# A transformer block on one core: the turn of the memory rows, the pace of the later projections, and the output steps behind the heads, in a table that sets the order of the work

## The chip, the cores and the metric

The kernel runs on one core of one Trainium2 chip. The metric is the device time of one execution, in microseconds (us), as the median of several runs. The kernel before took 1988.11 us, the median of 3 runs that lay between 1987.46 and 1988.55 us.

The engines are called as in the profile: PE is TensorE (matmuls), PEld its weight loads, DVE is VectorE, ACT is ScalarE, POOL is GpSimd, and SP is SyncE, which here only issues transfers from the chip's memory. Each engine takes its own instructions strictly in the order in which the program lists them.

## The reference

The reference is a transformer block with attention, cross attention to a memory and a gated feed-forward, then a second model of two more blocks. The change touches the first block's attention alone, which is this, cut to what matters:

```python
h = rmsnorm(x, attn_norm_g)                       # x: 512 tokens x 1024
fq, fk, fv, sq, sk, sv, f_logit = split(h @ w_in) # 8 + 8 heads of 64
log_f = log_sigmoid(f_logit + b_forget)
fox_o = softmax(fq.fk/8 + c[t] - c[s], causal) @ fv      # c = cumsum(log_f)
sb_o  = stick_breaking(sigmoid(sq.sk/8), strictly causal) @ sv
mixed = concat(rmsnorm(fox_o, fox_out_g), rmsnorm(sb_o, sb_out_g))
x = x + mixed @ w_out
h = rmsnorm(x, xattn_norm_g)
m = rmsnorm(mem, mem_norm_g)                      # mem: 256 rows x 1024
k, v = split(m @ w_mkv)                           # keys and values of the memory
x = x + softmax(heads(h @ w_mq).k/16) @ v @ w_mo
```

All of it is float32 in and out, to float32 accuracy.

## The kernel before

To reach that accuracy each float32 operand is split into two parts, high and low: ACT casts the high part (L162 for data, L179 for weights) and DVE subtracts it to get the low part (L163, L180). A product is then three matmuls (high by high, L197; high by low, L198; low by high, L199), called a step here. A step over 512 columns is three matmuls of 512 columns.

The stage that is changed is `mixers`, from about 45 us to 305 us of the span. It has two kinds of work. The first kind is projections, long chains of steps on PE that need little of the other engines: queries and keys of a pair of heads (`qk1` to `qk7`, 16 steps each), the values of the second eight heads (`v`, 32 steps), the keys of the memory (`mk`: two turns that only transpose the memory's rows, normalize and split them, then 32 turns of two steps over 256 columns), the memory's values (`mv`, 32 steps), and the output projection (`out`). The second kind is the sixteen heads, 0 to 7 stick-breaking and 8 to 15 with softmax and forget gates. A head's scores are eight small matmuls (L647, L648, over 128 to 512 columns) into two banks `ps_s`. ACT and DVE turn them into probabilities: for a softmax head DVE adds the bias and takes the maximum (L686), ACT exponentiates (L689), and POOL and DVE scale the rows (L257). Then PE transposes the ten blocks of probabilities (L417) into two banks `ps_t`, ACT and DVE split them again (`ch`, `cl`), and eight matmuls with the values follow (L706, L707) into one bank `ps_o`, which ACT and DVE empty at the end (L711, L712). Of a head the matmuls are short, and the other engines work on it for far longer than PE does.

The order is set by times without a unit. Head number h gives its four score rows between h - 0.68 and h + 0.106 and its products from h + 1.347 on. `FILL` is a list of projections with their number of turns and the time at which each ends, and within an entry the turns lie evenly. `weave` merges all these lanes by time into one program. From it a scheduler builds each engine's list of instructions by its own estimates, and may move an instruction ahead of others whose inputs it thinks late. So the order on an engine follows the table only roughly.

The memory's rows come in by two transfers (L778), issued by SP on the queue that also brings all weights (L174, into two buffers `wst`). Then 16 transposes (L538) put them into banks `ps_f`, of which there are three; the projections write to the same three. DVE scales each bank by the gain (L541) and the result is split. The rows wait for one of 13 large buffers `s8`. ACT squares the rows (L332) for their norms, and `spread` turns the norms into a row (L377 on DVE, L379 on PE). The first keys of the memory follow on PE after L379.

After `weave` the rest of `out` runs. Its last 36 of 64 steps need the softmax heads normalized, and that hangs on the last head: its squares are summed (L346, L347), split, summed over partitions by 8 small matmuls (L356, in `mean_sq`), raised to the power -1/2 on POOL (L319), spread to a row by 8 matmuls (L372), and multiplied in (L732). Meanwhile steps of `out` that need only the stick-breaking heads are there to run.

Of the kernel before, what the change touches and what calls it, by code (L numbers as in the profile page):

```python
# [13 lines left out]
F32R = mybir.dt.float32r  # L14
# [46 lines left out]
def weave(*lanes):  # L61

    heap = [(times[0], i, 0) for i, (times, _) in enumerate(lanes)]
    heapq.heapify(heap)
    while heap:
        t, i, k = heapq.heappop(heap)
        times, gen = lanes[i]
        if next(gen, None) is not None:
            k += 1
            heapq.heappush(heap, (times[min(k, len(times) - 1)], i, k))  # L70


def even(t0, t1, n):
    return [t0 + (i + 0.5) * (t1 - t0) / n for i in range(n)]


def filling(gens, plan, t0):

    times, parts = [], []
    for i, (name, n, t1) in enumerate(plan):  # L80
        times += even(t0, t1, n)
        more = any(name == later[0] for later in plan[i + 1:])
        parts.append(itertools.islice(gens[name], n) if more else gens[name])
        t0 = t1
    return times, itertools.chain(*parts)


def run(gen):
    for _ in gen:
        pass  # L90


FILL = [['qk1', 16, 0.85], ['qk2', 16, 2.1], ['qk3', 16, 3.4], ['v', 32, 5.95], ['qk4', 16, 7.2], ['qk5', 16, 8.5], ['qk6', 16, 9.85],
        ['mk', 2, 10.2], ['qk7', 16, 11.5], ['mk', 32, 13.9], ['mv', 32, 16.4], ['out', 12, 17.3]]
FOX_SCALE = 'pppd'
LATENT_SCALE = 'dpad'
NORM_SB = 14.0
# [9 lines left out]
class Kernel:  # L107
# [231 lines left out]
    def squares(self, acc, src, first):  # L339
# [6 lines left out]
        nc.scalar.activation(sq, src, AF.Square)  # L346
        nc.vector.tensor_add(acc, acc, sq)  # L347

    def mean_sq(self, acc, n, eps=EPS, bank="o"):

        ss = self.ps(bank)
        parts = [self.t2("sq", dt=F32R) for _ in range(2)]
        self.split(*parts, acc)
        for b in range(NB):
            for i, part in enumerate(parts):
                self.nc.tensor.matmul(ss[:, 2 * b:2 * b + 2], lhsT=part[:, b * P:(b + 1) * P], rhs=self.ones_r[:, 0:2],  # L356
                                      start=i == 0, stop=i == 1)
        ms = self.sm(NB)
        self.nc.vector.tensor_scalar(ms, ss[:, 0:2 * NB:2], 1.0 / n, eps, op0=ALU.mult, op1=ALU.add)  # L359
        return ms  # L360
# [355 lines left out]
    def mixers(self):  # L716

        a, nc = self.a, self.nc
        self.qk, self.rows = {}, {}
        cd = self.forget()  # L720
        self.sb_scale = self.scaled_cols(0.125)
        run(self.qk_pair(0))
        mixed, parts, v_fox = {}, {}, []
        accs = [self.t2("acc") for _ in range(2)]

        def split_mixed(kind, row):

            m = mixed[kind]
            parts[kind] = [self.s8([P, 4, T], F32R) for _ in range(2)]
            for pr in range(4):  # L730
                g = self.g[("sb", "fox")[kind]][:, pr:pr + 1]
                nc.vector.scalar_tensor_tensor(m[:, pr], m[:, pr], g, row, op0=ALU.mult, op1=ALU.mult)  # L732
                self.split(*(t[:, pr] for t in parts[kind]), m[:, pr])

        def normed_sb():
            row = self.spread(self.rstd_from(self.mean_sq(accs[0], 512, bank="f"), NB), "f")
            yield 1
            split_mixed(0, row)
            yield 1

        def values_fox():
            v_fox.extend(self.s8([P, NB, 4, 2, 64], F32R) for _ in range(2))
            for block in self.vproj(v_fox, 1024):
                yield from block


        out = self.down(lambda k: tuple(t[:, k % 4] for t in parts[k // 4]), a["w_out"][0], 8,
                        self.boundary(self.g["xattn"], rows=False),
                        [(range(3), range(4)), (range(3, 7), range(4)), (range(3), range(4, 8)), (range(3, 7), range(4, 8)),
                         ([7], range(4)), ([7], range(4, 8))], 2, row=lambda k: (k + 4) % 8)  # L750
        gens = {"mk": self.memory_keys(), "mv": self.memory_values(), "v": values_fox(), "out": itertools.islice(out, 12)}
        gens.update({f"qk{pr}": self.qk_pair(pr) for pr in range(1, 8)})
        lanes = [filling(gens, FILL, -0.4), ([NORM_SB, NORM_SB + 0.3], normed_sb())]
        for hd in range(16):
            kind = hd // 8
            v = (self.v_sb, v_fox)[kind]
            head = self.sb_head(hd) if kind == 0 else self.fox_head(hd, cd)
            lanes.append((even(hd + SCORES[0], hd + SCORES[1], 4), head))
            lanes.append(([hd + MIX_OUT + t for t in ATTEND], self.mix_head(hd, v, mixed, accs[kind])))
        weave(*lanes)  # L760
        self.x = [self.s8([P, 4, T]) for _ in range(2)]
        for h in range(2):
            nc.scalar.dma_start(self.x[h].rearrange("p k t -> p (k t)"), self.x_dram[h])
        run(itertools.islice(out, 7))
        ms = self.mean_sq(accs[1], 512)
        run(itertools.islice(out, 4))
        row = self.spread(self.rstd_from(ms, NB), direct=True)
        run(itertools.islice(out, 5))
        split_mixed(1, row)
        run(out)  # L770

# [603 lines left out]
```

## Time and profile before

| what | us |
|---|---|
| median of 3 runs | 1988.11 |
| profiled execution, its own time | 1992.29 |
| span of the profiled execution | 1990.5 |
| PE busy, of that span | 1955.9 |
| DVE busy | 1124.7 |
| ACT busy | 863.3 |
| POOL busy | 199.5 |

The profiled execution took 4.18 us more than the median of the runs. Its own time is 1.8 us longer than its span.

PE is busy for 98% of the span, and the chain that ended last runs for 94% of the span over PE. That makes PE the engine to follow, but its busy time has to be read with care: matmuls overlap each other, the profile models their ends, and a matmul that stands alone counts as busy for longer than the 0.23 us (512 columns) after which the next one could start. In stretches of short matmuls with waits between them, the busy share therefore hides lost time. Starts are the thing to look at there.

In forty slices of the span the granted PE clock shows 9 tenths or more everywhere. In finer windows the stage `mixers` has a few places where it is lower.

### The profile page before, as it was taken

The page shows a single profiled execution, that of the slowest core. Times are in us where ns is not written, and L with a number is a line of the kernel's source. Part 1 is how long each engine was busy: PE and PEld are TensorE (multiplying, and loading weights), DVE is VectorE, ACT ScalarE, POOL GpSimd, SP SyncE. Part 2 cuts the span into 40 slices and gives each one's busy share as a digit, 9 for nine tenths or more (in the row PEclk, how much of TensorE's full clock was granted, in tenths as well). Part 3 has the DMA queues.
Part 4 walks back from the last instruction along what each step waited for, and adds up shares of the span by engine and source line. Part 5 has one row for each costly group of instructions (what it writes and reads, how often), then busy time and mean ns, then how long its engine had stood idle before and what let it go on. Part 6 is the DMA issues. An engine that isn't in the chain of part 4 may idle for free.

```text
span 1990.5 us, 24467 instructions
## 1 busy us (share of the span) xinstructions
PE 1955.9 (98%) x9205; PEld 1634.4 (82%) x9205; DVE 1124.7 (57%) x1973; ACT 863.3 (43%) x1503; POOL 199.5 (10%) x260
## 2 busy tenths in 40 slices
PE   8999989999999999999999999999999999999998
PEld 7887978888888888888888888888887878888887
DVE  6788866567666533657775533333567764333334
ACT  6677744444333323645354323222446553332223
POOL 1545500001111100001210000000010000000000
PEclk9999999999999999999999999999999999999999
DMA  6323343123333332232223333223231123332332
GB/s 185 96 75 96 107 148 92 52 87 110 96 95 96 99 101 85 87 116 85 72 83 110 109 100 96 95 95 96 71 89 52 51 76 108 95 97 85 98 101 78
DMA packets 216344, 187.24 MB, mean 94 GB/s; under 512 B 12273, under 2 KB 188441, under 8 KB 215713
## 3 DMA queue, kind: packets, MB, share of 16 engines
q1 hardware_dynamic: 213905, 178.32, 30.1%
q10 hardware_dynamic: 2320, 7.36, 1.1%
q8 instruction: 72, 1.18, 0.3%
q14 instruction: 47, 0.39, 0.1%
HBM read 181.44 MB, written 4.21 MB: 93 GB/s over the span
## 4 chain that ended last, share of the span: by engine, by line
PE 94%; DVE 2%; ACT 2%; DMA 1%; issue 1%; POOL 0%; SPq 0%; ACTq 0%; POOLq 0%; DVEq 0%
PE ps_f L197 15%; PE ps_f L198 15%; PE ps_f L199 15%; PE ps_s L197 7%; PE ps_s L198 7%; PE ps_s L199 7%; PE ps_t L197 6%; PE ps_t L198 6%; PE ps_t L199 6%; PE ps_o L198 2%; PE ps_o L199 2%; PE ps_o L197 2%; PE ps_t L417 1%; ACT wh L179 0%; PE ps_s L647 0%
## 5 line engine op out<-in xcount | busy, mean ns | idle before, releaser
L179 ACT CAST wh<-wst 128x1024 fp32r<-128x1024 f32 (+4 forms) x349 | 344.1, 987 | 674.9 <-PE ps_f L198 317.9
L180 DVE TENSOR_TENSOR wl<-wst,wh 128x1024 fp32r<-128x1024 f32 (+4 forms) x349 | 401.2, 1150 | 325.7 <-ACT wh L179 319.6
L197 PE MATMUL ps_f<-s,wh 128*128 128x512 f32 (+1 forms) x892 | 344.0, 391 | 5.0 <-ACT s L162 2.5
L198 PE MATMUL ps_f<-s,wh 128*128 128x512 f32 (+1 forms) x892 | 344.7, 387 | 0.0
L199 PE MATMUL ps_f<-s,wl 128*128 128x512 f32 (+1 forms) x892 | 343.0, 386 | 0.0
L197 PEld LDWEIGHTS ps_f<-s,wh 128*128 128x128 f32 x892 | 168.8, 190 | 38.3 <-ACT s L162 2.9
L199 PEld LDWEIGHTS ps_f<-s,wl 128*128 128x128 f32 x892 | 169.2, 190 | 32.8 <-issue 0.2
L198 PEld LDWEIGHTS ps_f<-s,wh 128*128 128x128 f32 x892 | 169.5, 190 | 31.2 <-issue 0.5
L319 POOL TENSOR_TENSOR sm<-sm,m_half 128x1 f32<-128x1 f32 (+1 forms) x31 | 26.5, 855 | 1253.8 <-DVE sm L359 824.0
L162 ACT CAST ch<-s 128x512 fp32r<-128x512 f32 (+1 forms) x166 | 77.4, 496 | 154.1 <-PE ps_s L198 100.2
L163 DVE TENSOR_TENSOR cl<-s,ch 128x512 fp32r<-128x512 f32 (+1 forms) x166 | 85.8, 536 | 86.7 <-ACT ch L162 86.4
L197 PE MATMUL ps_s<-s,wh 128*128 128x512 f32 x288 | 112.8, 393 | 0.3 <-ACT wh L179 0.3
L198 PE MATMUL ps_s<-s,wh 128*128 128x512 f32 x288 | 112.4, 390 | 0.0
L199 PE MATMUL ps_s<-s,wl 128*128 128x512 f32 x288 | 111.8, 389 | 0.0
L197 PE MATMUL ps_t<-s,wh 128*128 128x512 f32 x280 | 109.4, 392 | 0.0
L198 PE MATMUL ps_t<-s,wh 128*128 128x512 f32 x280 | 109.1, 389 | 0.0
L199 PE MATMUL ps_t<-s,wl 128*128 128x512 f32 x280 | 108.3, 389 | 0.0
L198 PE MATMUL ps_f<-cl,wh 128*128 128x512 f32 x210 | 82.1, 391 | 0.0
L199 PE MATMUL ps_f<-ch,wl 128*128 128x512 f32 x210 | 81.8, 389 | 0.0
L197 PE MATMUL ps_f<-wh,s 128*128 128x512 f32 (+2 forms) x208 | 75.6, 374 | 3.5 <-ACT s L162 3.0
L198 PE MATMUL ps_f<-wl,s 128*128 128x512 f32 (+2 forms) x208 | 76.0, 369 | 1.0 <-DVE wl L180 1.0
L197 PE MATMUL ps_f<-ch,wh 128*128 128x512 f32 x210 | 76.4, 390 | 0.0
(452 smaller groups left out, 3902.2 us busy)
## 6 DMA issues: line engine op xcount, KB each, us to landing
wst<-in_mlp_w SPq DMA_DIRECT2D x128, 512.0 KB
wst<-in_w_up SPq DMA_DIRECT2D x44, 512.0 KB
wst<-in_a_w_in SPq DMA_DIRECT2D x32, 512.0 KB
wst<-in_w_in SPq DMA_DIRECT2D x23, 512.0 KB
wst<-in_w_down SPq DMA_DIRECT2D x22, 512.0 KB
wst<-in_w_mkv SPq DMA_DIRECT2D x16, 512.0 KB
wst<-in_a_w_out SPq DMA_DIRECT2D x16, 320.0 KB
wst<-in_w_mq SPq DMA_DIRECT2D x8, 512.0 KB
```

Of the source, the lines that this page charges most:

```text
L162: nc.scalar.copy(hi, src)
L163: nc.vector.tensor_sub(lo, src, hi.bitcast(F32))
L179: self.nc.scalar.copy(h[:, j], st[:, j])
L180: self.nc.vector.tensor_sub(l[:, j], st[:, j], h[:, j].bitcast(F32))
L197: mm(out, lhsT=ah, rhs=bh, start=first, stop=False)
L198: mm(out, lhsT=ah, rhs=bl, start=False, stop=False)
L199: mm(out, lhsT=al, rhs=bh, start=False, stop=last)
L319: self.nc.gpsimd.tensor_tensor(r, ms, self.m_half[:, 0:n], op=ALU.pow)
L417: self.nc.tensor.transpose(pt[:, i * P:(i + 1) * P], probs[i][:, j * P:(j + 1) * P], self.ident)
```

## The change

The table `FILL` is changed in four ways. The two turns that take in the memory's rows stood after `qk6` and before `qk7`; now they stand after `qk7`, at the head of the memory's keys (`mk`, 34 turns). The pairs end later: `qk5` at 8.8 instead of 8.5, `qk6` at 10.35 instead of 9.85, `qk7` at 11.8 instead of 11.5. The memory's keys end at 14.2, its values at 16.6. Of the output steps 8 instead of 12 lie among the heads, so that 20 instead of 16 lie behind them.

In the code behind `weave` the split of the last sum of squares is written ahead of the first of these steps (`split_acc`), and the steps come in pieces of 8, 6 and 6 instead of 7, 4 and 5.

```diff
-FILL = [['qk1', 16, 0.85], ['qk2', 16, 2.1], ['qk3', 16, 3.4], ['v', 32, 5.95], ['qk4', 16, 7.2], ['qk5', 16, 8.5], ['qk6', 16, 9.85],
-        ['mk', 2, 10.2], ['qk7', 16, 11.5], ['mk', 32, 13.9], ['mv', 32, 16.4], ['out', 12, 17.3]]
+FILL = [['qk1', 16, 0.85], ['qk2', 16, 2.15], ['qk3', 16, 3.5], ['v', 32, 6.1], ['qk4', 16, 7.3], ['qk5', 16, 8.8], ['qk6', 16, 10.35],
+        ['qk7', 16, 11.8], ['mk', 34, 14.2], ['mv', 32, 16.6], ['out', 8, 17.3]]
...
-    def mean_sq(self, acc, n, eps=EPS, bank="o"):
-
-        ss = self.ps(bank)
+    def split_acc(self, acc):
         parts = [self.t2("sq", dt=F32R) for _ in range(2)]
         self.split(*parts, acc)
+        return parts
+
+    def mean_sq(self, acc, n, eps=EPS, bank="o"):
+
+        ss = self.ps(bank)
+        parts = acc if isinstance(acc, list) else self.split_acc(acc)
...
-        run(itertools.islice(out, 7))
-        ms = self.mean_sq(accs[1], 512)
-        run(itertools.islice(out, 4))
+        acc = self.split_acc(accs[1])
+        run(itertools.islice(out, 8))
+        ms = self.mean_sq(acc, 512)
+        run(itertools.islice(out, 6))
         row = self.spread(self.rstd_from(ms, NB), direct=True)
-        run(itertools.islice(out, 5))
+        run(itertools.islice(out, 6))
```

Lines of the changed kernel behind `mean_sq` are 4 or 5 higher: its L542, L651, L652, L710, L711, L421 and L383 are the L538, L647, L648, L706, L707, L417 and L379 of before.

On PE, in the kernel before, the last of the 16 transposes of the memory's rows has passed and `qk7` begins (its steps read the normalized input, here `s_105` and `s_107`), between rows of two heads:

```order
L647 MATMUL ps_s<-s_1526 128x512
L648 MATMUL ps_s<-s_1526,ql 128x512
L707 MATMUL ps_o<-cl,s_111 128x128
L417 MATMUL ps_t<-ident_r,pp 128x128 x5
L647 MATMUL ps_s<-s_1717 128x128
L648 MATMUL ps_s<-s_1717,ql 128x128
L706 MATMUL ps_o<-ch,s_1130 128x512
L197 MATMUL ps_f<-s_105,wh 128x512
L198 MATMUL ps_f<-s_107,wh 128x512
L199 MATMUL ps_f<-s_105,wl 128x512
```

The rows down to L706 are the last of 79 matmuls and transposes in a row without a projection (two heads and the memory's rows). From L197 on `qk7`'s 48 matmuls lie among the rows of the next head, and then come 25 of a head without a projection, the first L379 as the last of them.

On PE, in the changed kernel, the end of `qk7` (reading `s_106`, `s_108`) and what follows it:

```order
L198 MATMUL ps_f<-s_108,wh 128x512
L710 MATMUL ps_o<-ch,s_111 128x256
L199 MATMUL ps_f<-s_106,wl 128x512
L651 MATMUL ps_s<-s_1539 128x128
L711 MATMUL ps_o<-cl,s_111 128x256
L710 MATMUL ps_o<-ch,s_111 128x128
L711 MATMUL ps_o<-cl,s_111 128x128
L421 MATMUL ps_t<-ident_r,pp 128x128 x4
L652 MATMUL ps_s<-s_1539,ql 128x128
L421 MATMUL ps_t<-ident_r,pp 128x128 x3
```

And, also on PE in the changed kernel, the next place at which a projection appears, the first keys of the memory (reading `s_2422`, `s_2423`, over 256 columns):

```order
L651 MATMUL ps_s<-s_1974 128x512
L652 MATMUL ps_s<-s_1974,ql 128x512
L651 MATMUL ps_s<-s_2190 128x128
L652 MATMUL ps_s<-s_2190,ql 128x128
L383 MATMUL ps_f<-sq,ones_r 128x256
L197 MATMUL ps_f<-s_2422,wh 128x256
L198 MATMUL ps_f<-s_2423,wh 128x256
L199 MATMUL ps_f<-s_2422,wl 128x256
```

Between these two places stand 159 matmuls and transposes without one of a projection: the scores of five heads and a row (heads 9 to 13, the first row of 14), 57 transposes of probabilities, the products of five heads, and the 16 transposes of the memory's rows, which begin about halfway. After the first 19 matmuls of the memory's keys and one score matmul come 125 in a row without a head.

On SP, in the kernel before, the memory's rows among the weights of the memory's keys (`in_w_mkv`, 128x8x128):

```order
L174 DMA wst<-in_w_in 128x2x512 x4
L174 DMA wst<-in_w_in 128x8x128 x8
L174 DMA wst<-in_w_mkv 128x8x128 x2
L778 DMA s_2146<-in_mem 128x1024 x2
L174 DMA wst<-in_w_mkv 128x8x128 x6
```

On SP in the changed kernel:

```order
L174 DMA wst<-in_w_in 128x2x512 x4
L174 DMA wst<-in_w_in 128x8x128 x8
L174 DMA wst<-in_w_mkv 128x8x128 x6
L783 DMA s_2419<-in_mem 128x1024 x2
L174 DMA wst<-in_w_mkv 128x8x128 x2
```

The rows are now issued behind six of these weights instead of two. They wait for the buffer of the normalized input's low part, which `qk7`'s keys read until their fourth of eight steps; the weight just ahead of them waits for the split of the fourth of `mk`'s weights, and that one waits for the last matmul of `qk7`.

## Rows read from the trace of the kernel before

**Rows 1.** The page: busy time of each engine, share of the span.

```profile
PE 1955.9 (98%) x9205; PEld 1634.4 (82%) x9205; DVE 1124.7 (57%) x1973; ACT 863.3 (43%) x1503; POOL 199.5 (10%) x260
```

**Rows 2.** Waits of PE, 150 to 330 us: us in total, times, longest.

```profile
PE ps_o L372 <- ACT sr L162: 2.6, 1, 2.6
PE ps_o L706 <- ACT ch L162: 2.4, 4, 1.0
PE ps_f L197 <- ACT s L162: 2.1, 1, 2.1
PE ps_o L706 <- DVE s L712: 1.8, 1, 1.8
```

**Rows 3.** Windows: length, busy PE, PEld, DVE, ACT, POOL, clock, DMA share, GB/s.

```profile
163.90:181.90 18.00, 13.51 (x80) 9.89 (x78) 16.32 (x42) 14.85 (x35) 15.41 (x25) 1.00 0.31 90
197.85:205.50 7.65, 6.03 (x26) 4.66 (x25) 6.59 (x20) 5.99 (x17) 5.04 (x8) 0.79 0.32 97
205.50:291.25 85.75, 84.57 (x518) 75.16 (x517) 67.06 (x147) 52.79 (x110) 26.13 (x31) 1.00 0.43 135
165.00:180.00 15.00, 11.94 (x70) 8.61 (x68) 13.39 (x38) 12.55 (x31) 12.89 (x21) 1.00 0.29 83
180.00:185.00 5.00, 3.55 (x8) 2.67 (x9) 4.94 (x11) 3.20 (x8) 3.30 (x5) 0.68 0.17 56
```

**Rows 4.** Timeline of PE, 163 to 184 us: start, length, instruction, idle before.

```profile
163.67 0.39 PE L199 MATMUL ps_f<-s,wl 128*128 128x512 f32 x1
...
164.63 0.95 PE L417 MATMUL ps_t<-ident_r,pp 128*128 128x128 f32 x7
165.33 0.36 PE L647 MATMUL ps_s<-s 128*128 128x256 f32 x1
...
167.15 0.47 PE L706 MATMUL ps_o<-ch,s 128*128 128x512 f32 x1 [0.46 <-ACT ch L162]
...
174.67 0.47 PE L706 MATMUL ps_o<-ch,s 128*128 128x512 f32 x1 [0.18 <-ACT ch L162]
...
181.28 0.47 PE L706 MATMUL ps_o<-ch,s 128*128 128x512 f32 x1 [1.79 <-DVE s L712]
181.91 0.79 PE L197 MATMUL ps_f<-s,wh 128*128 128x512 f32 x1 [0.17 <-DVE f L541]
```

**Rows 5.** Timeline of PE, 192 to 207 us.

```profile
192.61 0.39 PE L197 MATMUL ps_f<-s,wh 128*128 128x512 f32 x1
192.83 0.39 PE L198 MATMUL ps_f<-s,wh 128*128 128x512 f32 x1
...
198.09 0.39 PE L706 MATMUL ps_o<-ch,s 128*128 128x512 f32 x1
...
205.31 0.41 PE L379 MATMUL ps_f<-sq,ones_r 128*128 128x256 f32 x1
...
206.55 0.28 PE L199 MATMUL ps_f<-s,wl 128*128 128x256 f32 x1
206.67 0.28 PE L197 MATMUL ps_f<-s,wh 128*128 128x256 f32 x1
```

**Rows 6.** DVE in 164 to 206 us, by line and shape.

```profile
L163 DVE TENSOR_TENSOR s<-f,s 128x512 fp32r<-128x512 f32 x4 | 2.9, 736 | 0.2 <-ACT s L162 0.2
L541 DVE TENSOR_TENSOR f<-ps_f,gains 128x512 f32<-128x512 f32 x4 | 2.7, 686 | 0.0
```

**Rows 7.** Timeline of ACT, 168 to 170 us.

```profile
168.66 1.28 ACT L689 ACT_TABLE_LOAD   x1 [0.49 <-POOL pp L680]
```

**Rows 8.** Timeline of SP's queue: the memory's rows.

```profile
152.36 1.81 SPq L778 DMA_DIRECT2D s<-in_mem  x2
```

**Rows 9.** Timeline of ACT, DVE and PE after the last head, 284 to 292 us.

```profile
284.58 0.58 ACT L711 COPY s<-ps_o 64x512 f32<-64x512 f32 x1 [2.96 <-PE ps_o L707]
289.42 0.69 DVE L163 TENSOR_TENSOR sq<-acc,sq 128x512 fp32r<-128x512 f32 x1
291.25 0.95 PE L356 MATMUL ps_o<-ones_r,sq 128*128 128x2 f32 x8
```

More of the change, by code (lines that the diff above doesn't have):

```diff
@@ L347, in squares @@
         nc.vector.tensor_add(acc, acc, sq)
+    def split_acc(self, acc):
+        parts = [self.t2("sq", dt=F32R) for _ in range(2)]
+        self.split(*parts, acc)
+        return parts
     def mean_sq(self, acc, n, eps=EPS, bank="o"):
         ss = self.ps(bank)
-        parts = [self.t2("sq", dt=F32R) for _ in range(2)]
-        self.split(*parts, acc)
+        parts = acc if isinstance(acc, list) else self.split_acc(acc)
         for b in range(NB):
@@ L750, in mixers @@
                          ([7], range(4)), ([7], range(4, 8))], 2, row=lambda k: (k + 4) % 8)
-        gens = {"mk": self.memory_keys(), "mv": self.memory_values(), "v": values_fox(), "out": itertools.islice(out, 12)}
+        gens = {"mk": self.memory_keys(), "mv": self.memory_values(), "v": values_fox(), "out": itertools.islice(out, 8)}
         gens.update({f"qk{pr}": self.qk_pair(pr) for pr in range(1, 8)})
```

## The prediction

> **What bounds the kernel now.** I read the page first. PE is busy 98% of the span [rows 1], so time comes or goes only where PE is kept from work. Next I asked who makes PE wait in the stage that is changed. The long waits are few [rows 2]: two behind the last head, for the spread of its norm and for the input multiplied with it (2.6 and 2.1 us), and a group on the matmuls of heads with the values. Together they are some 9 us, and that is too small a picture of the loss. So I went to windows and to starts, which show what PE could have done.
>
> In the timeline a matmul of 512 columns follows the one before after 0.22 to 0.23 us, one of 256 columns after 0.12 us [rows 5], and seven transposes take 0.70 us from the first to the next instruction, 0.10 each [rows 4]. With 0.17 and 0.06 us for 384 and 128 columns (in proportion) I price each stretch that has no projection.
>
> Stretch A runs from the end of `qk6` (163.67 + 0.23 = 163.90) to the first matmul of `qk7` at 181.91 [rows 4], 18.0 us. Its 79 instructions are 43 transposes (4.3 us), 16 score matmuls (four of each width, 2.3 us) and 20 products (2.8 us), 9.4 us of work. So 8.6 us are lost. Stretch B runs from 197.85, where the next projection is cut off, to the L379 at 205.31 [rows 5], 7.5 us, for 10 transposes, six score matmuls, eight products and L379, 3.3 us of work. 4.1 us are lost. What is busy there is not PE: in A DVE is busy 16.3 of 18.0 us and POOL 15.4, in B DVE 6.6 of 7.65 [rows 3]. In both DVE sets the pace, with POOL and ACT close behind. From 205.50 on, where heads and projections lie mixed, PE is busy 84.6 of 85.75 us and DVE 67 [rows 3]. A head needs about 3 us of PE and twice that of DVE, so a head beside projections costs PE its 3 us, and a head without them costs what DVE takes.
>
> **The change part by part.** Stretches A and B go. Moving the memory's rows behind `qk7` means that nothing parts `qk6` from `qk7` any more, and the first matmul of `qk7` no longer waits for a bank that the rows' transposes filled (0.17 us behind L541, after 1.79 us behind L712 [rows 4]). That gives back 8.6 + 4.1 = 12.7 us, all of it lost time of A and B.
>
> One stretch comes in their place. The order has 159 instructions without a projection between the end of `qk7` and the first L379: 73 transposes (7.3 us), 42 score matmuls (ten each of 512, 384 and 256 columns, twelve of 128, 5.9 us), 43 products (6.0 us) and L379 (0.1 us), 19.3 us of work. How long it takes is the one large unknown. The nearest rows are the starts of a head's first product in A and B, since each head has one: 167.15, 174.67, 181.28 [rows 4], so 7.5 and 6.6 us from head to head. I take the stretch as the way to its first product (163.90 to 167.15 in A, 3.25 us), four periods of the mean 7.07 us, and from the last first product to L379 as in B (198.09 to 205.31, 7.2 us [rows 5]): 38.7 us. Two corrections: all four L541 and all four splits of the rows now lie inside, of which A had one each, so up to six DVE instructions of 0.69 or 0.74 us [rows 6] come in, 4 us at most; and the load of ACT's exponential table, 1.28 us in A [rows 7], falls into a place with projections, as does one weight split. I add 1.3 us and take 40 us. The loss is then 40 - 19.3 = 20.7 us.
>
> The bounds of these 40 us. From below: the shorter period, 6.6 us, with DVE's idle share of A squeezed out (16.3 of 18.0 busy) is 6.0 us; five of them and 3.25 us make 33.3 us. From above: four periods of 7.5 us and all 4 us of the rows make 44.5 us. I take 40 since both kinds of stretch are in it as they ran.
>
> A page speaks against such an order. The Trainium skill, "Perfetto Trace Analysis", section Optimization Strategy, says that a kernel may have regimes with different most-contended engines, and that interleaving these may gain. This case's windows show two such regimes, and the change sets them further apart: five heads alone, then 144 matmuls of the memory's keys with one score matmul among them. The page has no price, and the sum here uses none of it.
>
> Clock: after A the granted clock is 0.68 from 180 to 185 us [rows 3], that is, the lower of the two levels (1.2 GHz) until about 185, and in B the mean is 0.79. At the end of the new stretch I expect the same low start once; one fall is saved and the other stays, which I cost at nothing, since the fall of B lies inside its 7.5 us. The bound below is 0, and above 1.6 us for one more fall (5 us at 0.68 instead of 1).
>
> The transfer of the memory's rows. SP issues two DMAs, 1.8 us of issue [rows 8], and in the new order they stand behind a weight that waits for the end of `qk7`. Behind them on SP wait the last weights of the memory's keys. First use is the transposes, which stand about half of the stretch in, some 20 us after that. The slack covers any transfer of 1 MB here, so nothing. If heads ran twice as fast it would be late too, and the gain below would be smaller.
>
> After the stretch 144 matmuls of 256 columns run for 17 us with little from the heads; DVE and ACT are free and PE is the bound. From there to the end of the heads the same work is left for PE in both kernels but for the two heads that are already done, at its own pace. Nothing.
>
> The tail. Of the 20 output steps four come from among the heads, and PE does them either way. In both orders all output steps that are ready stand ahead of L356, so the waits of 2.6 and 2.1 us behind it stay. What covers the last head's squares changes: 30 matmuls stand between its last product and L356 before, 25 after (5.7 us). The chain from L711 to the split's low part runs from 284.58 to 290.11, 5.5 us, and L356 starts at 291.25 without a wait [rows 9]. In the new order a weight split of DVE stands ahead of the last sum instead of behind it; ACT's part starts 1 us later for it and ends as late, since DVE does the same work in all. So the split written ahead brings nothing, and 0.2 us of slack is left. Bounds: 0 and +1.2 us (the weight split in full).
>
> Sum: 20.7 - 12.7 = +8.0 us. On the profiled execution's own 1992.29 us that is 2000.3. The runs' median is 4.18 us below the profiled execution, which is the profiling's and not the change's, so the forecast is 1988.11 + 8.0 = 1996.1 us. With the bounds of the stretch alone: 33.3 us gives +1.3, 44.5 us gives +12.5, and with one more fall of the clock and a late tail +15.3.
>
> **The rivals.** First, no change: in one long run of heads DVE has always another head's work to take, its waits close, and the stretch takes 33 us or a little more. For it: five heads in a row leave no beginning and no end of a stretch between them. Against it: the order on DVE is fixed, and its gaps in A are waits for ACT within a head. Time: 1988.1 + 1.3 = 1989.4.
>
> Second, faster: the heads without projections run nearly at PE's pace. The place is the same stretch, the price is the 12.7 us that go, and the point from which it decides is a stretch of 32 us (19.3 + 12.7). For it: part of A's and B's periods is work of the pairs and weights, not of heads, which has projections beside it now (B holds a weight split and the row's spread). If a period without that work were 5 us, the stretch would be 3.25 + 5 x 5 + 1.3 = 29.6 us, 2.4 us below that point: 1985.7. If no time at all were lost in it, 1975.4. Against it: DVE is 91% busy in A and POOL 86%.
>
> Third, the clock falls inside the long stretch and keeps falling. For it: in A it held at 1.00 from 165 to 180 with PE about half at work, and fell behind one wait of 1.79 us [rows 3, 4]; the new stretch has four such waits, one per head. At half rate PE's 19.3 us of work would be 38.6, as long as the stretch itself, and a head's chain through PE longer. Priced as three falls of 1.6 us: 1996.1 + 4.8 = 2000.9. The Trainium skill, "TensorE: Matmul & The Clock Gate", section A second HAM failure mode: psum-queue depth-cycling, tells of a kernel that swung between the two rates since PE idled briefly between groups; by that rule this would be the likelier case. In A's 15 us at 1.00 the trace does not bear it out.
>
> **How the numbers follow.** A measurement of this kernel tells 0.2%, 4 us, from no change. I give the forecast 0.54, the clock 0.17, no change 0.18, faster 0.11. Of the forecast 0.05 lies under +4 us (a stretch under 36 us), and of the faster case 0.02 within -4 us. So slower by over 0.2%: 0.66 (0.49 + 0.17); within: 0.25 (0.18 + 0.05 + 0.02); faster: 0.09. The range runs from the no-change side and the small gain to the clock's falls, 1986.5 to 2002.5; the forecast's own range is 1990 to 2002.
>
> **What would show it.** In the changed profile, between the last matmul of `qk7` and the first L383, a stretch of 36 to 44 us without a projection, DVE about 90% busy and PE's starts of 128x512 products 6.6 to 7.5 us apart, five of them; then 17 us of 256-column matmuls back to back while DVE is half idle. The waits behind the last head stay at 2.6 and 2.1 us, and there is no wait for the memory's rows at the transposes. I am wrong if the stretch is 32 us or shorter, if PE waits there for the transfer, or if the gain of A and B is not there because projections wait elsewhere.

## The result and the profile after

The changed kernel takes 2003.35 us (median of 4 runs, 2000.0 to 2005.18) against 1988.33 us of the kernel before, run beside it. These two medians lie 15.0 us apart. The ratio on record is 1.0062, 95% interval 1.005 to 1.0074, which is 12.3 us; the four runs of before beside the result were among its quicker ones, and 68 more of its runs in the groups below have a median of 1990.8 us. So I take about 12.3 us slower. The forecast was 8.0 us slower. The profiled execution took 2004.7 us (span 2003.0), 12.4 us over that of before.

The page's first line, where [rows 1] stood, shows PE's busy time 6.4 us longer for the same 9205 matmuls:

```profile
PE 1962.3 (98%) x9205; PEld 1638.0 (82%) x9205; DVE 1125.0 (56%) x1973; ACT 864.6 (43%) x1503; POOL 194.3 (10%) x260
```

The waits of PE from 150 to 330 us (us in total, times, longest) answer to [rows 2]. Waits among the heads have grown, and one on L383 is new; the two behind the last head are 3.0 and 2.1 us.

```profile
PE ps_o L710 <- ACT ch L162: 4.6, 3, 2.5
PE ps_s L651 <- DVE sm L690: 3.6, 5, 1.0
PE ps_o L376 <- ACT sr L162: 3.0, 1, 3.0
PE ps_f L197 <- ACT s L162: 2.1, 1, 2.1
PE ps_o L711 <- DVE cl L163: 1.8, 2, 1.4
PE ps_f L383 <- DVE sq L381: 1.3, 1, 1.3
```

Windows (columns as in [rows 3]): the stretch without projections, the memory's keys behind it, then two windows at a second place, and the long stretch in pieces of 5 us.

```profile
177.90:222.00 44.10, 33.52 (x160) 25.48 (x159) 34.87 (x109) 31.42 (x84) 29.52 (x46) 0.81 0.18 61
222.00:248.10 26.10, 26.10 (x215) 25.88 (x215) 19.31 (x44) 14.47 (x30) 5.87 (x8) 1.00 0.39 122
249.90:253.60 3.70, 1.34 (x5) 0.82 (x5) 3.43 (x9) 3.43 (x10) 0.04 (x1) 0.84 0.30 89
253.60:259.10 5.50, 5.50 (x14) 4.27 (x13) 2.95 (x10) 0.76 (x3) 1.54 (x2) 0.50 0.28 91
...
195.00:200.00 5.00, 4.05 (x20) 2.72 (x21) 3.42 (x15) 3.04 (x10) 3.28 (x5) 1.00 0.20 50
200.00:205.00 5.00, 3.87 (x19) 3.11 (x18) 4.87 (x12) 4.23 (x10) 4.79 (x8) 0.62 0.00 0
205.00:210.00 5.00, 3.81 (x14) 2.85 (x14) 5.00 (x14) 2.67 (x7) 1.92 (x5) 0.50 0.06 21
210.00:215.00 5.00, 2.44 (x11) 1.72 (x10) 2.73 (x10) 4.31 (x14) 3.96 (x6) 0.84 0.09 32
```

The timeline of PE answers to [rows 4, 5]: the end of `qk7`, the five first products of a head (L710, 512 columns), the rows' transposes (L542), L383, the first matmul of the memory's keys, and the second place.

```profile
177.65 0.40 PE L199 MATMUL ps_f<-s,wl 128*128 128x512 f32 x1
...
180.99 0.47 PE L710 MATMUL ps_o<-ch,s 128*128 128x512 f32 x1
...
187.29 0.61 PE L710 MATMUL ps_o<-ch,s 128*128 128x512 f32 x1 [0.29 <-DVE s L716]
...
192.07 1.06 PE L542 MATMUL ps_f<-ident_r,s 128*128 128x128 f32 x8
194.96 0.51 PE L710 MATMUL ps_o<-ch,s 128*128 128x512 f32 x1 [1.83 <-ACT ch L162]
...
203.99 0.79 PE L710 MATMUL ps_o<-ch,s 128*128 128x512 f32 x1
...
215.05 0.79 PE L710 MATMUL ps_o<-ch,s 128*128 128x512 f32 x1 [2.53 <-ACT ch L162]
...
221.80 0.39 PE L383 MATMUL ps_f<-sq,ones_r 128*128 128x256 f32 x1
222.02 0.28 PE L197 MATMUL ps_f<-s,wh 128*128 128x256 f32 x1
...
251.04 0.44 PE L651 MATMUL ps_s<-s 128*128 128x384 f32 x1 [1.03 <-DVE sm L690]
...
252.98 0.80 PE L383 MATMUL ps_f<-sq,ones_r 128*128 128x512 f32 x1 [1.32 <-DVE sq L381]
253.58 0.63 PE L197 MATMUL ps_f<-wh,s 128*128 128x512 f32 x1
```

The one long stretch is there: from 177.88 (177.65 + 0.23) to L383 at 221.80, 43.9 us. At 250 us there is a loss that the prediction did not have: two waits of 1.0 and 1.3 us, and then, the clock at 0.50, 5.5 us for thirteen matmuls that take 3.0 at full rate. The second of these waits is for the spread of the norm of the first eight heads (L383). In the kernel before the same matmul, there L379, stands among projections and waits for nothing:

```profile
253.06 0.39 PE L379 MATMUL ps_f<-sq,ones_r 128*128 128x512 f32 x1
```

For a ledger I take the time between the starts of two neighbouring PE instructions and subtract what the first takes at full rate (0.2325, 0.174, 0.119 and 0.06 us for 512, 384, 256 and 128 columns, 0.10 for a transpose or a matmul of 2 columns). What is left is lost time, from waits or from the clock. It is summed over pieces that begin and end at the same work in both kernels; a stretch is counted from the start of the last projection matmul ahead of it to the first one behind.

| piece | before | after |
|---|---|---|
| stretches without projections | 8.6 (A) + 4.3 (B) | 24.7 |
| between A and B, and up to 256 (before); 222 to 248 (after) | 2.8 | 0.3 |
| around the norm of the first eight heads (256 to 264; 248 to 262) | 1.8 | 5.9 |
| the tail | 8.3 | 9.0 |
| rest | 0.5 | -0.4 |
| sum | 26.4 | 39.4 |

The difference, 13.0 us, is the 12.5 us of the spans but for rounding in the prices. The stretches cost 11.8 us more, the second place 4.1 us more, and 2.5 us are won between.

### The profile page after: what moved, and what is told of

It reads as the page before. It is cut to its first block, busy times and chain, and to the rows that moved or that the text cites. A ratio compares the mean times of both kernels' runs of the same rounds, so it can differ in the third digit from the quotient of the medians.

```text
span 2003.0 us, 24474 instructions
## 1 busy us (share of the span) xinstructions
PE 1962.3 (98%) x9205; PEld 1638.0 (82%) x9205; DVE 1125.0 (56%) x1973; ACT 864.6 (43%) x1503; POOL 194.3 (10%) x260
## 4 chain that ended last, share of the span: by engine, by line
PE 93%; DVE 2%; ACT 2%; DMA 1%; issue 1%; POOL 0%; SPq 0%; ACTq 0%; POOLq 0%; DVEq 0%
PE ps_f L197 15%; PE ps_f L198 15%; PE ps_f L199 15%; PE ps_s L197 7%; PE ps_s L198 7%; PE ps_s L199 6%; PE ps_t L197 6%; PE ps_t L198 6%; PE ps_t L199 6%; PE ps_o L198 2%; PE ps_o L199 2%; PE ps_o L197 2%; PE ps_t L421 1%; ACT wh L179 1%; DVE wl L180 1%
## 5 line engine op out<-in xcount | busy, mean ns | idle before, releaser
L197 PE MATMUL ps_f<-s,wh 128*128 128x512 f32 (+1 forms) x892 | 342.5, 389 | 4.8 <-ACT s L162 2.4
L197 PEld LDWEIGHTS ps_f<-s,wh 128*128 128x128 f32 x892 | 168.4, 189 | 37.2 <-ACT s L162 2.9
L197 PE MATMUL ps_s<-s,wh 128*128 128x512 f32 x288 | 112.8, 393 | 0.3 <-ACT wh L179 0.3
L197 PE MATMUL ps_t<-s,wh 128*128 128x512 f32 x280 | 109.4, 392 | 0.0
L197 PE MATMUL ps_f<-wh,s 128*128 128x512 f32 (+2 forms) x208 | 76.9, 379 | 3.3 <-ACT s L162 2.8
L199 PE MATMUL ps_f<-wh,s 128*128 128x512 f32 (+2 forms) x208 | 76.5, 372 | 0.0
```

Source lines behind the costliest of these rows:

```text
L197: mm(out, lhsT=ah, rhs=bh, start=first, stop=False)
L199: mm(out, lhsT=al, rhs=bh, start=False, stop=last)
```

## The experiments

Each ratio is to the kernel before, run on the same chip beside the group; the experiments stand in groups of four. Before alone had medians of 1988.3, 1990.8, 1991.8 and 1990.7 us beside the result and the three groups, so that between groups differences of 0.001 to 0.002 say little. Lost times are by the ledger's count.

### The change taken apart (first group)

`e1_rows_back` keeps all of the change but the place of the memory's rows:

```diff
-        ['qk7', 16, 11.8], ['mk', 34, 14.2], ['mv', 32, 16.6], ['out', 8, 17.3]]
+        ['mk', 2, 10.55], ['qk7', 16, 11.8], ['mk', 32, 14.2], ['mv', 32, 16.6], ['out', 8, 17.3]]
```

> All of the change stays but one thing: the memory's rows are turned ahead of qk7 again. In the order the stretch of 159 instructions without a projection (19.3 us of work) is gone; one of 106 (12.7 us of work) lies ahead of qk7 and one of 30 (3.5 us) behind the memory's keys, against 79 and 25 (9.4 and 3.3 us) before. Theory (projection-free stretches cost about as much again as their work, since heads alone go at DVE's pace): 16.2 us of such work against 12.7 before, so 3 to 4 us over before, 1991 to 1993, and some 10 us under the changed kernel. Rival (the tail or the later output steps cost the time): as slow as the changed kernel, about 2001. Rival (the clock alone): 1988 to 1990, since two stretches were there before as well.

Measured: 1986.94 us, ratio 0.9985 (0.9977 to 0.9994), faster than before, which no theory had said. Its stretch and PE's instructions around the rows:

```profile
163.70:189.20 25.50, 20.09 (x106) 15.71 (x105) 21.78 (x64) 19.18 (x48) 22.07 (x35) 0.87 0.31 105
```

```profile
186.35 1.07 PE L542 MATMUL ps_f<-ident_r,s 128*128 128x128 f32 x8
...
188.45 1.04 PE L542 MATMUL ps_f<-ident_r,s 128*128 128x128 f32 x8
189.24 0.47 PE L197 MATMUL ps_f<-s,wh 128*128 128x512 f32 x1
```

The stretch loses 12.7 us for 13.0 of work, as much as A and B together (12.9), and B's place loses nothing more. Here the rows stand at the end of the stretch, and 2.9 us behind their first transpose PE is at the next projection (186.35 to 189.24), since `qk7` needs nothing of the rows. In the changed kernel the next projection is the memory's own and needs the rows turned, split and normed: 192.07 to 222.02, 30 us.

`e2_move_only` is before with the rows moved and nothing else:

```diff
-        ['mk', 2, 10.2], ['qk7', 16, 11.5], ['mk', 32, 13.9], ['mv', 32, 16.4], ['out', 12, 17.3]]
+        ['qk7', 16, 11.5], ['mk', 34, 13.9], ['mv', 32, 16.4], ['out', 12, 17.3]]
```

> Before with the one edit that the memory's rows are turned behind qk7; times of the other projections, 12 output steps and the tail as before. The order has one stretch of 151 instructions without a projection (18.6 us of work). Theory: nearly the whole loss is here, 22 to 24 us lost in the stretch against 12.7, so +9 to +12 us, 1997 to 2000. Rival (the tail or the stretched times cost it): 1988 to 1990.

Measured: 1999.88 us, ratio 1.0048 (1.0035 to 1.0061), as the theory had it. Its stretch, from the last matmul of `qk7` to the first of the memory's keys, is 42.5 us (23.4 lost):

```profile
178.49 0.40 PE L199 MATMUL ps_f<-s,wl 128*128 128x512 f32 x1
...
220.95 0.28 PE L197 MATMUL ps_f<-s,wh 128*128 128x256 f32 x1
```

It has no second place: 0.7 us are lost from the stretch to 270 us.

`e3_tail_only` is before with the change's tail, `e4_times_only` before with its times (those of the pairs up to `qk6` as in the change, and the line shown):

```diff
-        ['mk', 2, 10.2], ['qk7', 16, 11.5], ['mk', 32, 13.9], ['mv', 32, 16.4], ['out', 12, 17.3]]
+        ['mk', 2, 10.2], ['qk7', 16, 11.5], ['mk', 32, 13.9], ['mv', 32, 16.4], ['out', 8, 17.3]]
...
+        acc = self.split_acc(accs[1])
+        run(itertools.islice(out, 8))
+        ms = self.mean_sq(acc, 512)
...
```

> Before with the tail of the change alone: 20 output steps behind the heads in groups of 8, 6 and 6, and the last squares split ahead. Stretches of 79 and 25 instructions as before. Theory: 25 instead of 30 matmuls still cover the squares, 0 (at most +1.2), 1988 to 1989.5. Rival (the tail costs the time): 1995 to 2001.

```diff
-        ['mk', 2, 10.2], ['qk7', 16, 11.5], ['mk', 32, 13.9], ['mv', 32, 16.4], ['out', 12, 17.3]]
+        ['mk', 2, 10.55], ['qk7', 16, 11.8], ['mk', 32, 14.2], ['mv', 32, 16.6], ['out', 12, 17.3]]
```

> Before with the stretched times of the pairs alone, the memory's rows still ahead of qk7. The order is that of the kernel with the rows put back, stretches of 106 and 30 instructions. Theory: +3 to +4 us, 1991 to 1993, the same as the kernel with the rows put back within 1 us. Rival (the times only shift work that PE does either way): 1988.

Measured: the tail 1991.9 us, 1.0005 (0.9996 to 1.0014), nothing. The times 1987.22 us, 0.9987 (0.9978 to 0.9996), a gain where the theory had a loss of 3 to 4 us. My count by the work of a stretch was wrong: it gave this kernel 16.2 us of work alone against 12.7 and hence a loss, but the second of its two runs of heads (30 instructions) lost only 2.1 us.

So by the ratios the move costs nearly 10 us by itself, and the times gain 2.6 us without it. With it they bring nothing; the changed kernel is at 1.0062, not at 1.0048 - 0.0013.

### What the lost time is made of (second group)

`e5_filled` adds work that nobody reads: the last key projection four times more, with 32 more turns for it in the table.

```diff
-        ['qk7', 16, 11.8], ['mk', 34, 14.2], ['mv', 32, 16.6], ['out', 8, 17.3]]
+        ['qk7', 48, 11.8], ['mk', 34, 14.2], ['mv', 32, 16.6], ['out', 8, 17.3]]
...
+        for _ in range(4 if pr == 7 else 0):
+            yield from self.tform(self.ps("f"), ws[1], n["xT"], 8)
```

> The changed kernel with work added: the key projection of the last pair is done four times more, into banks that nobody reads (96 matmuls of 512 columns, 21.8 us of work at full rate). In the order six pieces of it now lie among the heads that stood alone, and 83 instructions (9.8 us of work) of them are still without a projection. Theory (heads alone wait for DVE, and PE's idle time there takes other work): the first half of the heads goes beside the added matmuls at no loss, what is left loses about as rows-back's stretch did, 9 to 12 us instead of 24.7; so 21.8 us of added work cost only 7 to 10 us over the changed kernel, ratio to before 1.009 to 1.012. Granted clock 1.00 beside the added matmuls. Rival (the stretch is long by its own work on PE or by the memory's rows): +18 to +22 us over the changed kernel, ratio 1.015 to 1.018.

Measured: 2007.81 us, ratio 1.0085 (1.0071 to 1.0098), so 21.8 us of added work cost 4.6 us over the changed kernel, less than the 7 to 10 expected (each ratio is good to about 2.5 us). Windows: the added matmuls with heads among them, and the heads still alone.

```profile
175.90:209.60 33.70, 33.70 (x178) 28.77 (x177) 18.67 (x57) 15.81 (x42) 16.70 (x25) 1.00 0.18 61
209.60:230.80 21.20, 14.56 (x86) 11.24 (x85) 16.97 (x49) 15.28 (x40) 13.07 (x21) 0.97 0.17 49
```

In the first PE is never idle and the clock stays at 1.00; 0.3 us are lost. In the second 11.1 us are lost for 10.1 of work. PE's idle time in the stretch took other work: the rival, at 1.015 or more, is out.

`e6_norm_late` and `e7_act_scales` are the changed kernel with one number, and one letter, changed:

```diff
-NORM_SB = 14.0
+NORM_SB = 14.6
```

> The changed kernel with one number changed, the time at which the norm of the first eight heads is given out, 14.0 to 14.6. The order of the long stretch of 159 instructions stays; the norm's column sums move 7 us of work later and its two spread matmuls lie among the memory's values. Theory (the second loss in the changed profile, two waits of 1.0 and 1.3 us at 250 to 253 and the half clock until 259, is the chain of this norm with no projection ahead of it, 3.3 us more than before lost there): 2.5 to 4.5 us faster than the changed kernel, ratio to before 1.004 to 1.005. Rival (the heads run out of projections there whatever the norm does): no change, 1.0062.

```diff
-FOX_SCALE = 'pppd'
+FOX_SCALE = 'pppa'
```

> The changed kernel with one of DVE's instructions per head moved to ACT: the scaling of the 512-column row of the probabilities (0.49 to 0.81 us on DVE in the changed profile). The order has the same long stretch (161 instructions). Theory (DVE alone sets the pace of heads without projections): five heads by some 0.65 us, 2 to 3.5 us faster than the changed kernel, ratio 1.0045 to 1.005. Rival (the pace is a chain through ACT, DVE, POOL and PE, and PE's longest waits there are for ACT's copies of the transposes): no gain or a loss of up to 2 us, ratio 1.006 to 1.007.

Measured: the late norm 1998.2 us, 1.0035 (1.0023 to 1.0048), a little more gain than the theory had. The place at 250 us is gone, and the stretch is still there:

```profile
178.70:221.80 43.10, 31.18 (x160) 23.39 (x159) 35.08 (x109) 31.32 (x84) 29.91 (x46) 0.88 0.18 63
245.00:260.00 15.00, 15.00 (x89) 13.09 (x88) 12.60 (x33) 9.92 (x23) 6.66 (x9) 1.00 0.42 141
```

The scales on ACT: 1998.07 us, 1.0036 (1.0023 to 1.0048). The gain looks like the theory's, but the trace says otherwise:

```profile
177.10:220.90 43.80, 31.46 (x162) 24.56 (x161) 33.46 (x107) 34.55 (x91) 29.75 (x47) 0.88 0.20 61
250.80:256.00 5.20, 5.20 (x24) 4.28 (x23) 4.22 (x12) 2.15 (x5) 1.54 (x2) 1.00 0.30 104
```

The stretch is as long as before that edit (44.1 against 44.4 us by the ledger), with 1.4 us less on DVE and 3.1 more on ACT. What is won is at the second place, which now loses 1.8 us instead of 5.9, since PE goes on at full clock there. Taking work from DVE and giving it to ACT does not shorten heads that stand alone: the theory that DVE alone sets their pace falls. What less work on both would do is not shown.

`e8_rows_back_norm_late` joins what gained: `e1_rows_back` with the norm at 14.6.

> The kernel with the memory's rows put back ahead of qk7 (ratio 0.9985), and the norm of the first eight heads given out at 14.6 instead of 14.0. In the order the second stretch of 30 instructions (3.5 us of work) is gone. Theory: the 1.6 us lost there go, ratio 0.997 to 0.998. Rival: the norm's chain is as late elsewhere, 0.9985.

Measured: 1985.0 us, ratio 0.9968 (0.9956 to 0.9979), by the ratio 6.4 us faster than before and the fastest version found. Windows: its stretch, and all from there to the tail.

```profile
163.80:189.30 25.50, 20.14 (x108) 15.70 (x106) 21.80 (x64) 19.22 (x48) 22.05 (x35) 0.87 0.33 105
189.30:287.00 97.70, 97.70 (x588) 86.63 (x587) 78.69 (x178) 64.77 (x137) 30.89 (x40) 1.00 0.45 135
```

Behind the stretch PE is busy 97.70 of 97.70 us.

### Can it go further, and what fills the stretch (third group)

`e9_rows_back_norm_late_act` is that kernel with `FOX_SCALE = 'pppa'`, `e10_before_norm_late` before with `NORM_SB = 14.6`.

> The fastest kernel so far (rows back ahead of qk7, norm at 14.6; ratio 0.9968) with the 512-column scaling of each head moved from DVE to ACT. Moving it left the changed kernel's long stretch at its length (44.1 against 44.4 us) and gained behind it. Theory (the stretch is a chain through all engines, so the move gains nothing in it, and there is no second loss left here): 0.996 to 0.998, no different from 0.9968. Rival (DVE's load counts): four heads by some 0.65 us and what follows, 0.995.

> The kernel before with one number changed, the time of the first eight heads' norm, 14.0 to 14.6. Stretches of 79 and 25 instructions as before. Theory: before loses little beside that norm, 1.8 us lost at 256 to 264 may go: 0.999 to 1.000; the gain of the fastest kernel is then from the projections' times (0.9987 alone) and from the norm only where those put a stretch beside it. Rival (the norm's time is the gain itself): 0.9985 or less.

Measured: 1988.98 us, 0.9994 (0.9985 to 1.0003), so with the scales on ACT nearly all that the other edits won is lost, which neither the theory nor the rival had. In the trace the stretch loses 13.2 instead of 12.7 us, and far behind it, at 261 us, 1.3 us go, where a projection waits for DVE behind a head's product. That is some 2 us; the rest of the step from 0.9968 is unexplained, and part of it may be between the groups. The norm alone on before: 1988.98 us, 0.9991 (0.9981 to 1.0), as expected.

`e11_narrow_norm` shortens the Squares that ACT takes of the memory's rows, in the kernel of `e6_norm_late`:

```diff
-            nc.vector.tensor_copy(col[:, b:b + 1], self.block_rstd(st[:, b]))
+            nc.vector.tensor_copy(col[:, b:b + 1], self.rstd([st[:, b, 0:64], st[:, b, 512:576]], D, [self.t2("sq")[:, 0:64] for _ in range(2)]))
```

> The changed kernel with the norm at 14.6 (ratio 1.0035, stretch 43.3 us), and the squares of the memory's rows taken over 128 of their 1024 elements: four Squares of ACT (0.62 us each) are a fraction of that. The norm of the memory's rows is then not that of the reference. The order's stretch is 169 instructions (20.8 us of work) instead of 159 (19.3). Theory (those Squares stand on ACT ahead of a copy that PE waits for, the 2.5 us wait at 212 to 215 in the changed profile): that wait is under 1.2 us, stretch 42 to 44 us in spite of 1.5 us more work, ratio 1.0025 to 1.004. Rival (the heads' own chain sets the time, whatever ACT does for the rows): the stretch grows with its work, 45 to 47 us, ratio 1.0045 to 1.0055.

The row behind this: in the changed kernel's timeline of ACT the Squares stand ahead of the copy `ch`, for which PE waits until 215.05.

```profile
212.46 0.62 ACT L332 ACTIVATE sq<-s 128x512 f32<-128x512 f32 x1
...
213.68 0.62 ACT L332 ACTIVATE sq<-s 128x512 f32<-128x512 f32 x1
...
214.42 0.97 ACT L162 CAST ch<-ps_t 128x512 fp32r<-128x512 f32 x2
```

Measured: 1996.21 us, 1.0026 (1.0017 to 1.0036), stretch 45.1 us. The time is as the theory had it, its mechanism is not: PE's wait is 2.01 us, not under 1.2, and the stretch lies in the rival's 45 to 47. The same place in this run:

```profile
212.03 0.24 ACT L332 ACTIVATE sq<-s 128x64 f32<-128x64 f32 x1
...
212.80 0.26 ACT L332 ACTIVATE sq<-s 128x64 f32<-128x64 f32 x1 [0.44 <-DVE sm L336]
...
213.41 0.97 ACT L162 CAST ch<-ps_t 128x512 fp32r<-128x512 f32 x2
```

The third Square now waits for DVE, and ACT's copy stands behind it all the same. So the length of the Squares did not set PE's wait here. What did is not shown, and the test is inconclusive on the size, since 10 more instructions came into the stretch.

`e12_rows_ahead_of_qk6` turns the rows a pair earlier than `e8_rows_back_norm_late`:

```diff
-FILL = [['qk1', 16, 0.85], ['qk2', 16, 2.15], ['qk3', 16, 3.5], ['v', 32, 6.1], ['qk4', 16, 7.3], ['qk5', 16, 8.8], ['qk6', 16, 10.35],
-        ['mk', 2, 10.55], ['qk7', 16, 11.8], ['mk', 32, 14.2], ['mv', 32, 16.6], ['out', 8, 17.3]]
+FILL = [['qk1', 16, 0.85], ['qk2', 16, 2.15], ['qk3', 16, 3.5], ['v', 32, 6.1], ['qk4', 16, 7.3], ['qk5', 16, 8.8], ['mk', 2, 9.0], ['qk6', 16, 10.35],
+        ['qk7', 16, 11.8], ['mk', 32, 14.2], ['mv', 32, 16.6], ['out', 8, 17.3]]
```

> The fastest kernel so far, with the memory's rows turned one pair earlier, ahead of qk6. In the order the stretch of 106 instructions (12.7 us of work) becomes two of 53 and 37 (6.0 and 4.9 us). Theory (a stretch loses more than its share the longer it is: 13.3 us lost for 12.4 of work, 25.3 for 19.1, but 4.3 for 3.6): two short ones lose 8 to 11 us, so 2 to 5 us faster, ratio 0.9945 to 0.996. Rival (what is lost goes by the work that stands alone, whatever its division, and each stretch has its own clock fall): 0.9965 to 0.998.

Measured: 1988.48 us, 0.9987 (0.9978 to 0.9996), slower than the theory and the rival had it. (The losses of 13.3 and 25.3 us in the expectation price the 16 transposes of the rows at 0.06 us; at the ledger's 0.10 they are 12.7 and 24.7.) Windows of its two stretches:

```profile
149.50:158.30 8.80, 7.88 (x54) 6.41 (x52) 7.48 (x15) 7.47 (x15) 4.10 (x9) 1.00 0.22 62
187.60:201.80 14.20, 9.45 (x39) 6.95 (x39) 12.49 (x37) 11.73 (x32) 10.85 (x18) 0.80 0.18 56
```

They lose 2.8 us for 6.2 of work and 9.2 us for 5.2, together 12.0 in place of 12.7. Two short stretches are hardly better than a long one; the theory of lengths falls, and so does a price that goes by PE's work alone. Besides, the tail loses some 2.7 us more than that of `e8_rows_back_norm_late`, with a wait of 1.5 us for ACT ahead of L360.

## Why the prediction was right or wrong

**The direction and the cause held.** PE bounds the kernel, and the time went where PE was kept from work: one stretch of 159 instructions in place of A and B. The move alone costs 1.0048, the rows put back undo it. Of the ledger's 13.0 us the prediction had 8.0; what it missed is 3.9 us in the stretch and 4.1 at a place that it did not price, set off in part by 2.5 us that it did not expect to win. The median of 2003.35 us lies 0.9 above its range; by the ratio, on the 1988.11 us it started from, the change is 2000.4 and inside. By the Trainium skill, "Perfetto Trace Analysis", section Optimization Strategy, regimes with different most-contended engines may gain by being interleaved; the added projections of `e5_filled`, 21.8 us of work for 4.6 us, agree.

**The stretch was mis-sized by 3.9 us**: 43.9 measured, 40 forecast (bounds 33.3 and 44.5). The starts above give 3.1 us to the first product, periods of 6.30, 7.67, 9.03 and 11.06, and 6.75 to L383. The three without the rows' splits have a mean of 6.9 us, where the prediction took 7.07 and 7.2. The other two, from 194.96 to 215.05, hold the rows' work and are 6.3 us longer than two such periods. The step that failed is "I add 1.3 us" for the rows: it counted up to six DVE instructions, 4 us at most (A in fact holds two L541, at 172.25 and 181.16), and set the table load and a weight split against them. All eight of the rows on DVE are there, 5.9 us, and ACT does eight more, 5.0 us (lines of 177.9 to 222 us):

```profile
L163 DVE TENSOR_TENSOR s<-f,s 128x512 fp32r<-128x512 f32 x4 | 3.2, 795 | 0.1
...
L545 DVE TENSOR_TENSOR f<-ps_f,gains 128x512 f32<-128x512 f32 x4 | 2.7, 683 | 0.1
```

```profile
L332 ACT ACTIVATE sq<-s 128x512 f32<-128x512 f32 x4 | 2.5, 623 | 0.0
L162 ACT CAST s<-f 128x512 fp32r<-128x512 f32 x4 | 2.5, 619 | 2.2 <-DVE f L545 2.1
```

That these delays come from the rows' chain as a whole is read from the trace; `e11_narrow_norm` did not single out a part of it. In `e1_rows_back`, where the rows' transposes come last in the stretch, the first products start at 167.08, 174.05 and 179.53, 7.0 and 5.5 us apart. The fall of the clock is not what makes the first of these two periods long: in `e6_norm_late` it is 8.84 us with the clock at 1.00 until 205 us. The second, 11.05 us there, has a fall in it in both runs.

```profile
194.96 0.50 PE L710 MATMUL ps_o<-ch,s 128*128 128x512 f32 x1 [1.49 <-ACT ch L162]
...
203.80 0.49 PE L710 MATMUL ps_o<-ch,s 128*128 128x512 f32 x1 [0.71 <-ACT ch L162]
...
214.85 0.79 PE L710 MATMUL ps_o<-ch,s 128*128 128x512 f32 x1 [2.34 <-ACT ch L162]
```

```profile
200.00:205.00 5.00, 2.68 (x19) 2.02 (x18) 4.87 (x12) 4.14 (x10) 4.79 (x8) 1.00 0.00 0
```

**"DVE sets the pace" was wrong**, though the price taken from its periods was near. DVE is busy 34.87 of 44.10 us, 79%, not the 90% forecast, and `e7_act_scales` took work from it for nothing. PE waits there for ACT and for DVE by turns, which fits a chain through PE, ACT, DVE and POOL; no run isolates that chain.

**"The same work is left for PE: nothing" was wrong** by 4.1 us less the 2.5 us won. Behind the stretch the memory's keys ran back to back, as forecast (26.10 of 26.10 us busy), but so closely packed that none was left to cover the norm of the first eight heads. The edit of its time (`e6_norm_late`) took that place away and was worth 0.0027 in the ratio.

**The clock**, rival three, did what it said: after 1.00 from 195 to 200 us, 0.62, 0.50 and 0.84 follow. The price was smaller. With a mean of 0.88 instead of 0.81 the stretch of `e6_norm_late` is 1.1 us shorter by the ledger; not the 4.8 us of that rival, and the forecast's 0 is nearer. Where it did cost was behind the second place, 2.5 us. The Trainium skill, "TensorE: Matmul & The Clock Gate", section A second HAM failure mode: psum-queue depth-cycling, tells of such a swing between the rates; the trace agrees on the swing, 0.50 to 1.00 within the stretch; what it cost here are the 1.1 and 2.5 us just told.

**The offset of 4.18 us** between the profiled execution of before and its median is put down to the profiling in the prediction. That execution ran at a mean granted clock of 0.993, and 14 runs of before at 0.993 have a median of 1992.8 us against its 1992.29: the offset goes with the clock. The forecast of +8.0 us does not rest on it.

**Held as forecast:** the transfer is hidden. SP's queue shows it 28 us later than in [rows 8], 11.5 us ahead of the first L542, and PE waits there for no transfer.

```profile
180.53 1.00 SPq L783 DMA_DIRECT2D s<-in_mem  x2
```

The tail is even: 1.0005 alone, its waits 3.0 and 2.1 us against 2.6 and 2.1 in [rows 2]. The rivals "no change" and "faster" needed a stretch of 33 or 32 us and are out.

## What to carry to other kernels

Ask not only what a moved step leaves behind, but what the next filler needs: work that feeds the next filler must be done while another filler, which does not need it, still runs. Price every instruction of the moved step on every engine that the waiting chain crosses, and look for the short chains (a norm, a spread) that were covered by what you pack together. An engine that is the busiest of a stretch, here at 79%, may still not be its pace alone; moving one instruction off it is a test.

## What the runs showed of the hardware

The run time of one kernel goes with the mean granted clock of the run. Over 68 runs of the kernel before, the median is 1992.8 us at a mean clock of 0.993 (14 runs), 1990.6 at 0.995 (16 runs) and 1986.9 at 0.997 (3 runs). These medians span 5.9 of the 8.0 us between its fastest and slowest run (1986.1 to 1994.1). The changed kernel's four runs go the same way, 2000.0 us at 0.994 and 2004.7 at 0.989. At 0.993 and 0.994 it is 8 to 9 us over runs of before at the same clock (2002.0 against 1992.8, 2000.0 against 1991.8). So some 3 to 4 us of its 12.3 seem to go with its lower clock, an estimate from four runs. In the profiled run that lower clock is made at the change's own places: 0.81 over the 44.1 us of the stretch and 0.50 over 5.5 us behind the second place take 0.0056 off the mean of the span, where 0.68 over 5 us and 0.79 over 7.65 us [rows 3] take 0.0016 in the kernel before. The difference is that of the two means, 0.989 and 0.993.
